# Channel norm of a convolution branch placed behind the fifth of eight attention half pairs of `w_out`, with the conv gates made ahead of it

## Chip, cores and metric

The kernel runs on one core of one Trainium2 chip. The metric is the device time of one execution in microseconds; 0.2% of it (4.4 us) is about what a measurement of this kernel can tell from no change. Engines are called PE (TensorE), DVE (VectorE), ACT (ScalarE), POOL (GpSimd) and SP (SyncE, which issues the weight loads). Every engine works through its own list of instructions in order.

## What is computed

The reference is two blocks on 256 tokens of width 2048, all in float32. The change lies in the first block, which has two layers. One layer, cut to what matters here:

```python
u = _rmsnorm(h, norm_g[i]) @ w_in[i]
a_val, a_glu, a_z, q, k, v, b_z = split(u)
y  = depthwise_conv31(a_val * sigmoid(a_glu)) + conv_b      # 1024 channels
ya = silu(layernorm_over_channels(y, cln_g, cln_b)) * silu(a_z)
yb = window_attention(q, k, v) * silu(b_z)                  # 1024 columns
h  = h + concat([ya, yb]) @ w_out[i]
e  = _rmsnorm(p[i] @ w_pe[i], pe_g[i])
h  = h + e * sigmoid(h @ w_pg[i])
```

The product with `w_out` has two halves of rows: the conv half needs `ya`, the attention half needs `yb` alone.

## The kernel before

Activations lie transposed, channels on partitions and 256 tokens along the free axis. Weights come from HBM in tiles of 4 x 128 rows by 256 columns (512 KB, SP). ACT rounds each to a high part (`whi`, L285), DVE forms the rest (`wlo`, L286), each from a pool of three buffers. Activations are kept as high and low parts as well (`Split`, `split_pair`, L271 and L272). `wide` makes one pair of output tiles: 16 k-tiles for `w_in`, 8 for one half of `w_out`. A half pair of `w_out` is thus two weight tiles: 16 matmuls of 512 columns (L353) and 16 of 256 (L355). `add_wide` (L368) adds the result to the residual `hT` in four DVE instructions.

A layer in program order: values and gates of the conv, keys, values, then four times queries, attention and two channel tiles of the convolution (30 DVE instructions each, L591, into `cy`); then the **channel norm**: `cs` sums the eight channel tiles over partitions on PE (L597), DVE subtracts the mean (L601), ACT squares (L603, L606), DVE adds (L607, L224), PE reduces to two columns (`pc`, L227), DVE makes the reciprocal root in thirteen small instructions (L207 to L214), copies it out (`rbx`, L246), PE transposes it (`rbp`, L249), ACT copies it to `rl` (L251). Then four z pairs of `w_in` with their `silu`, each followed by its two tiles of `cy` times `rl` (L616), `silu` (L619), times z (L621), split into `Y` (L271, L272). Then the eight attention half pairs of `w_out`, after every second of them one part of the embedding (`embed_part`: one weight tile of `w_pe`, 24 matmuls of 256 columns, L1231 to L1233, a square on ACT (L404), `ev` (L749) and a write of `ev` to the DRAM table `etab` by POOL, L750). Then `embed_scale` (`pc`, root and `rbp` of the embedding's own norm, into `re`), and the eight conv half pairs, which read `Y`.

The work isn't run in that order: the framework's scheduler places each instruction on its engine at build, by priorities that fall along the program's text (weight loads and splits are raised by `HP`). In the order before, the z pairs and the first four and a half attention half pairs stand ahead of the end of the convolution on PE. Below, "half pair a0 to a7" is an attention half pair, "b0" the first conv half pair, "e1 to e4" the four parts of the embedding.

Of the kernel before, what the change touches and what calls it, by code (L numbers as in the profile page):

```python
# [8 lines left out]
F32 = mybir.dt.float32  # L9
F32R = mybir.dt.float32r  # L10
I32 = mybir.dt.int32
AF = mybir.ActivationFunctionType
ALU = mybir.AluOpType
# [5 lines left out]
SEQ = 256  # L19
EPS = 1e-6  # L20
# [71 lines left out]
def bc(ap, n):  # L92

    p, x = ap.shape
    return ap.unsqueeze(1).to_broadcast([p, n, x])
# [21 lines left out]
class Kern:  # L117
# [395 lines left out]
    def layer1(self, i, S, st):  # L513
        nc, A = self.nc, self.A
        w_in = A["w_in"][i]
        kall = list(range(KD))
        if i == 0:
            rc, r = st
        else:
            rc = self.rs_cols(st["acc"], 1.0 / D, EPS, "rcl")  # L520
            r = self.bcast(rc[:], "r")
        r2 = bc(r[:], 2)
        cy = self.w1.tile([128, 8, SEQ], F32, tag="cy", name=self.nm("cy"))
# [13 lines left out]
        V = self.v1[i]  # L537
# [22 lines left out]
        Y = self.new_split()  # L560
        tail = None

        for j in range(4):
# [20 lines left out]
            for t in range(2):  # L584
                c = 2 * j + t
                cw = V["conv_w"][c]
                y = cy[:, c, :]
                ap = apads[j]
                nc.scalar.activation(y, ap[:, t, 0:SEQ], AF.Identity, scale=cw[:, 0:1], bias=V["conv_b"][:, c : c + 1])
                for k in range(1, 31):  # L590
                    prev, tail = tail, nc.vector.scalar_tensor_tensor(y, ap[:, t, k : k + SEQ], cw[:, k : k + 1], y, ALU.mult, ALU.add)  # L591
                    if k == 1 and prev is not None:
                        self.behind(tail, prev)

        ss = self.psum("o", [128, SEQ], "cs")
        for c in range(8):
            nc.tensor.matmul(ss[:], lhsT=self.ones, rhs=cy[:, c, :], start=(c == 0), stop=(c == 7))  # L597
        acc = self.wk.tile([128, 2, SEQ], F32, tag="acc", bufs=self.accb, name=self.nm("lnacc"))
        for c in range(0, 8, 2):
            y = cy[:, c : c + 2, :]  # L600
            nc.vector.scalar_tensor_tensor(y, bc(ss[:], 2), -1.0 / 1024, y, ALU.mult, ALU.add)  # L601
            if c == 0:
                nc.scalar.activation(acc[:], y, AF.Square)  # L603
            else:
                sq = self.w1.tile([128, 2, SEQ], F32, tag="sq", name=self.nm("sq"))
                nc.scalar.activation(sq[:], y, AF.Square)  # L606
                nc.vector.tensor_tensor(acc[:], acc[:], sq[:], ALU.add)  # L607
        rl = self.bcast(self.rs_cols(acc, 1.0 / 1024, EPS, "rc")[:], "rl", pool=self.w1)
        for j in range(4):
            pz = self.wide(w_in, 0, kall, 2048 + j * 256, S)  # L610
            zz = self.wk.tile([128, 2, SEQ], F32, tag="s", bufs=4, name=self.nm("z"))
            self.fold(zz, pz)
            nc.vector.tensor_tensor(zz[:], zz[:], r2, ALU.mult)
            nc.scalar.activation(zz[:], zz[:], AF.Silu)
            y = cy[:, 2 * j : 2 * j + 2, :]
            nc.vector.tensor_tensor(y, y, bc(rl[:], 2), ALU.mult)  # L616
            for t in range(2):
                c = 2 * j + t
                nc.scalar.activation(cy[:, c, :], cy[:, c, :], AF.Silu, scale=V["cln_g"][:, c : c + 1],  # L619
                                     bias=V["cln_b"][:, c : c + 1])  # L620
            nc.vector.tensor_tensor(y, y, zz[:], ALU.mult)  # L621
            self.split_pair(Y, 2 * j, y)

        for j in range(8):
            ps = self.wide(A["w_out"][i], 0, list(range(8, 16)), j * 256, Y)
            hh = self.at(self.hT, 2 * j, 2)
            self.add_wide(hh, ps)
            if j % 2:
                self.embed_part(i, j // 2, E)
        if self.dbg and f"yT{i}" in self.dbg:  # L630
            pass
        etab, re = E["tab"], self.embed_scale(E)
# [30 lines left out]
                self.stat_add(self.stf, hh, [self.fg[:, 2 * j + t : 2 * j + t + 1] for t in range(2)])  # L663
        self.dump_h(f"hT{i}")
        return N, st2

    def attend1(self, i, j, q, vd, gz, Y):
        nc = self.nc
# [917 lines left out]
```

## Time and profile before

| | us |
|---|---|
| median of 3 runs (2212.31 to 2216.68) | 2216.26 |
| the profiled execution, its own time | 2216.77 |
| its span | 2213.8 |
| PE busy in the span | 2168.2 (98%) |
| DVE busy | 1711.1 (77%) |
| ACT busy | 1207.7 (55%) |

The span starts at 0 with the first instruction; times of the trace are us from there, and some 3 us of the execution lie outside. The timeline merges neighbouring instructions of one line and gives in brackets how long the engine stood idle ahead of a row and what ended that. The windows give each engine's busy time in a stretch and the clock that TensorE was granted there, as a share of full speed.

### The profile page before, as it was taken

Reading aid. Unit: us, or ns where it says so; the run is one execution under the profiler, and the core shown is the slowest. Engines: PE = TensorE matmul, PEld = TensorE weight load, DVE = VectorE, ACT = ScalarE, POOL = GpSimd, SP = SyncE. Lnnn points to the kernel's source line nnn. Section 1 sums busy time; section 2 is a strip of 40 time slices with the busy share of each in tenths; the row PEclk is TensorE's granted clock in tenths of the full one; section 3 lists DMA queues with packets and bytes.
Section 4 is the critical chain, followed back from the end, with each engine's and each line's share of the span. In section 5 each row is a group of like instructions: output and inputs, shape, how many; then the busy total and the mean of one; then the engine's idle time right before and its main releaser. Section 6 shows DMA issues by size and latency. Waiting matters only on the chain.

```text
span 2213.8 us, 36348 instructions
## 1 busy us (share of the span) xinstructions
PE 2168.2 (98%) x13687; PEld 1935.8 (87%) x13687; DVE 1711.1 (77%) x3176; ACT 1207.7 (55%) x1861; POOL 106.4 (5%) x253
## 2 busy tenths in 40 slices
PE   8999999999999999999999999999999999999997
PEld 7899988888899878899999888888888888888887
DVE  6999999778989889787787877776765576556765
ACT  6456636565566546665666556455443444444443
POOL 3100000000000000001100000020000000000000
PEclk9999999999999999999999999999999999999999
DMA  8875556666665457677774435476666666566654
GB/s 238 240 211 164 173 162 209 194 207 189 188 183 170 149 166 219 212 214 216 221 183 123 129 88 158 157 255 203 191 189 192 194 189 190 190 196 188 189 190 140
DMA packets 374511, 412.76 MB, mean 186 GB/s; under 512 B 40456, under 2 KB 327429, under 8 KB 373952
## 3 DMA queue, kind: packets, MB, share of 16 engines
q1 hardware_dynamic: 336464, 366.06, 54.4%
q0 software_dynamic: 10960, 31.79, 4.6%
q10 hardware_dynamic: 26912, 12.60, 2.4%
q8 instruction: 107, 1.75, 0.3%
q14 instruction: 68, 0.56, 0.1%
HBM read 390.47 MB, written 19.92 MB: 185 GB/s over the span
## 4 chain that ended last, share of the span: by engine, by line
PE 91%; DVE 3%; DMA 2%; ACT 2%; issue 1%; ACTq 1%; SPq 0%; DVEq 0%
PE wide L353 35%; PE wide L355 18%; PE lin L328 4%; PE lin L327 4%; PE lin L329 4%; PE lin L1401 3%; PE lin L1402 3%; PE lin L1400 3%; PE dn L1402 2%; PE dn L1401 2%; PE dn L1400 2%; PE po L709 1%; DVE wlo L286 1%; PE lin L1231 1%; PE lin L1232 1%; PE lin L1233 1%
## 5 line engine op out<-in xcount | busy, mean ns | idle before, releaser
L285 ACT CAST whi<-wraw 128x1024 fp32r<-128x1024 f32 (+1 forms) x708 | 725.2, 1027 | 670.6 <-PE wide L353 290.8
L286 DVE TENSOR_TENSOR wlo<-wraw,whi 128x1024 fp32r<-128x1024 f32 (+1 forms) x708 | 843.4, 1192 | 313.6 <-ACT whi L285 307.0
L353 PE MATMUL wide<-xs,whi 128*128 128x512 f32 x3492 | 853.0, 393 | 6.0 <-ACT whi L285 3.7
L353 PEld LDWEIGHTS wide<-xs,whi 128*128 128x128 f32 x3492 | 638.0, 189 | 129.8 <-ACT whi L285 5.3
L355 PEld LDWEIGHTS wide<-xs,wlo 128*128 128x128 f32 x3492 | 454.2, 191 | 25.8 <-DVE wlo L286 5.5
L355 PE MATMUL wide<-xs,wlo 128*128 128x256 f32 x3492 | 466.3, 284 | 3.6 <-DVE wlo L286 3.6
L327 PE MATMUL lin<-xs,whi 128*128 128x256 f32 x844 | 241.1, 286 | 1.2 <-ACT whi L285 0.6
L329 PE MATMUL lin<-xs,wlo 128*128 128x256 f32 x844 | 240.2, 285 | 1.6 <-DVE wlo L286 1.6
L328 PE MATMUL lin<-xs,whi 128*128 128x256 f32 x844 | 240.2, 285 | 0.0
L591 DVE SCALAR_TENSOR_TENSOR cy<-apad,vc_cw,cy 128x256 f32<-128x256 f32 x480 | 229.6, 480 | 6.7
L327 PEld LDWEIGHTS lin<-xs,whi 128*128 128x128 f32 x844 | 161.5, 191 | 2.7 <-ACT whi L285 0.8
L329 PEld LDWEIGHTS lin<-xs,wlo 128*128 128x128 f32 x844 | 161.5, 191 | 2.4 <-DVE wlo L286 1.8
L328 PEld LDWEIGHTS lin<-xs,whi 128*128 128x128 f32 x844 | 161.6, 191 | 1.1 <-issue 0.7
L1401 PE MATMUL lin<-wlo,xs 128*128 128x512 f32 (+1 forms) x304 | 117.4, 386 | 0.5 <-DVE wlo L286 0.5
L1402 PE MATMUL lin<-whi,xs 128*128 128x512 f32 (+1 forms) x304 | 117.0, 385 | 0.0
L1400 PE MATMUL lin<-whi,xs 128*128 128x512 f32 (+1 forms) x304 | 113.7, 386 | 1.2 <-ACT whi L285 1.2
L1400 PEld LDWEIGHTS lin<-whi,xs 128*128 128x128 f32 x304 | 57.1, 188 | 12.8 <-ACT whi L285 1.6
L1401 PEld LDWEIGHTS lin<-wlo,xs 128*128 128x128 f32 x304 | 57.2, 188 | 11.9 <-DVE wlo L286 1.0
L1400 PE MATMUL dn<-whi,xs 128*128 128x512 f32 (+1 forms) x176 | 67.0, 381 | 0.0
L1401 PE MATMUL dn<-wlo,xs 128*128 128x512 f32 (+1 forms) x176 | 67.0, 381 | 0.0
L1402 PE MATMUL dn<-whi,xs 128*128 128x512 f32 (+1 forms) x176 | 67.0, 381 | 0.0
L1402 PEld LDWEIGHTS lin<-whi,xs 128*128 128x128 f32 x304 | 57.1, 188 | 11.1
(544 smaller groups left out, 2401.1 us busy)
## 6 DMA issues: line engine op xcount, KB each, us to landing
wraw<-in_w_in_dram SPq DMA_DIRECT2D x244, 512.0 KB, 4.1
wraw<-in_w_out_dram SPq DMA_DIRECT2D x89, 512.0 KB, 4.0
wraw<-in_ffn_w_gate_dram SPq DMA_DIRECT2D x88, 512.0 KB, 4.1
wraw<-in_ffn_w_up_dram SPq DMA_DIRECT2D x88, 512.0 KB, 3.9
wraw<-in_ffn_w_down_dram SPq DMA_DIRECT2D x87, 512.0 KB, 4.3
wraw<-in_w_pg_dram SPq DMA_DIRECT2D x64, 512.0 KB, 4.5
bt<-btab POOLq DMA_DIRECT2D x32, 192.0 KB, 3.1
btab<-bF ACTq DMA_DIRECT2D x4, 1024.0 KB, 8.1
```

Of the source, the lines that this page charges most:

```text
L285: nc.scalar.copy(hi[:], src)
L286: self.lo = nc.vector.tensor_tensor(lo[:], src, hi[:].bitcast(F32), ALU.subtract)
L327: nc.tensor.matmul(ps[:, t, :], lhsT=h, rhs=xh_, start=((t, k) == first), stop=False)
L328: nc.tensor.matmul(ps[:, t, :], lhsT=h, rhs=xl_, start=False, stop=False)
L329: nc.tensor.matmul(ps[:, t, :], lhsT=l, rhs=xh_, start=False, stop=((t, k) == last))
L353: nc.tensor.matmul(ps[t][:], lhsT=hi[:, i, ts], rhs=S.both(k).rearrange("p u c -> p (u c)"), **flags)
L355: nc.tensor.matmul(ps[t][:, :SEQ], lhsT=lo[:, i, ts], rhs=S.hi(k), **flags)
L591: prev, tail = tail, nc.vector.scalar_tensor_tensor(y, ap[:, t, k : k + SEQ], cw[:, k : k + 1], y, ALU.mult, ALU.add)
L709: nc.tensor.matmul(po[:, qb, g, :], lhsT=pT[:, kb, qb * 128 : qb * 128 + 128], rhs=vd[:, kb, j, :], start=(kb == 0), stop=(kb == 1))
L1400: nc.tensor.matmul(ps, lhsT=zh, rhs=hi, start=(k == 0), stop=False)
L1401: nc.tensor.matmul(ps, lhsT=zh, rhs=lo, start=False, stop=False)
L1402: nc.tensor.matmul(ps, lhsT=zl, rhs=hi, start=False, stop=(k == nt - 1))
```

## The change

The four z pairs move ahead of the norm, and their four gates stay in the four buffers of the tag `s`. The norm moves into a function, `channel_norm`, which the text calls behind attention half pair a4 (`j == 4`); applying it to `cy` (times `rl`, `silu`, times z, split) moves behind the last attention half pair and the last embedding part. No instruction of the arithmetic is added or dropped.

```diff
-        ss = self.psum("o", [128, SEQ], "cs")
...
-        rl = self.bcast(self.rs_cols(acc, 1.0 / 1024, EPS, "rc")[:], "rl", pool=self.w1)
+        zs = []
         for j in range(4):
             pz = self.wide(w_in, 0, kall, 2048 + j * 256, S)
...
             nc.scalar.activation(zz[:], zz[:], AF.Silu)
+            zs.append(zz)
+
+        for j in range(8):
+            ps = self.wide(A["w_out"][i], 0, list(range(8, 16)), j * 256, Y)
+            hh = self.at(self.hT, 2 * j, 2)
+            self.add_wide(hh, ps)
+            if j % 2:
+                self.embed_part(i, j // 2, E)
+            if j == 4:
+                rl = self.channel_norm(cy)
+        for j in range(4):
             y = cy[:, 2 * j : 2 * j + 2, :]
             nc.vector.tensor_tensor(y, y, bc(rl[:], 2), ALU.mult)
...
-            nc.vector.tensor_tensor(y, y, zz[:], ALU.mult)
+            nc.vector.tensor_tensor(y, y, zs[j][:], ALU.mult)
             self.split_pair(Y, 2 * j, y)
-
-        for j in range(8):
...
+    def channel_norm(self, cy):
+
+        nc = self.nc
+        ss = self.psum("o", [128, SEQ], "cs")
+        for c in range(8):
+            nc.tensor.matmul(ss[:], lhsT=self.ones, rhs=cy[:, c, :], start=(c == 0), stop=(c == 7))
...
+        return self.bcast(self.rs_cols(acc, 1.0 / 1024, EPS, "rc")[:], "rl", pool=self.w1)
```

In the changed program lines behind the edit have other numbers: the mean is L666, the squares L668 and L671, `cy` times `rl` L613, its `silu` L616, times z L618, the embedding matmuls L1239 to L1241, `ev` L757.

On PE in layer 0 the last channel sum `cs` (the one that needs the convolution's last instruction) stands, before, between the two halves of embedding part e2 (`lin_3547` and `lin_3567`):

```order
L1231 MATMUL lin_3547<-pp_2340,whi_3543 128x256
L1232 MATMUL lin_3547<-pp_2340,whi_3543 128x256
L1233 MATMUL lin_3547<-pp_2340,wlo_3544 128x256
L597 MATMUL cs_2834<-cy_261,cblk 128x256
L1231 MATMUL lin_3567<-pp_2340,whi_3543 128x256
L1232 MATMUL lin_3567<-pp_2340,whi_3543 128x256
```

and now inside embedding part e3 (`lin_3669`, `lin_3689`), behind half pairs a4 and a5:

```order
L1241 MATMUL lin_3669<-pp_2340,wlo_3666 128x256
L1240 MATMUL lin_3689<-pp_2340,whi_3665 128x256
L1241 MATMUL lin_3689<-pp_2340,wlo_3666 128x256
L1239 MATMUL lin_3689<-pp_2340,whi_3665 128x256
L662 MATMUL cs_3562<-cy_261,cblk 128x256
L1240 MATMUL lin_3689<-pp_2340,whi_3665 128x256
```

The same sum has moved behind half of e2, half of a4, all of a5 and 14 matmuls of e3. On PE in layer 0, at the end of the stretch, the last part of the embedding (`lin_3859`) is followed directly by the first conv half pair (`wide_3935`, `wide_3936`, which read `Y` as `xs_1330`) before:

```order
L1231 MATMUL lin_3859<-pp_2340,whi_3835 128x256
L1232 MATMUL lin_3859<-pp_2340,whi_3835 128x256
L1233 MATMUL lin_3859<-pp_2340,wlo_3836 128x256
L353 MATMUL wide_3936<-xs_1330,whi_3941 128x512 x2
L353 MATMUL wide_3935<-xs_1330,whi_3941 128x512 x4
```

and now there stand between them the embedding's `pc_3879` and two transposes, `rbp_3608` of the channel norm and `rbp_3901` of the embedding:

```order
L1240 MATMUL lin_3835<-pp_2340,whi_3811 128x256
L1241 MATMUL lin_3835<-pp_2340,wlo_3812 128x256
L227 MATMUL pc_3879<-cblk,acc_2343 128x1 x2
L249 MATMUL rbp_3608<-cblk,rbx_3606 128x128 x2
L249 MATMUL rbp_3901<-cblk,rbx_3899 128x128 x2
L189 MATMUL vps_4351<-cblk,vst_3906 128x124
L353 MATMUL wide_3935<-xs_1330,whi_3941 128x512 x2
```

Before, `rbp` of the channel norm stood ahead of a6 and the embedding's `pc` and `rbp` among the conv half pairs; the norm's own `pc` now stands right behind a7 in layer 0 and inside a7 in layer 1. On ACT in layer 0 the square of the norm's first pair (`lnacc`) stood before ahead of the square and the `ev` that read the embedding's `lin_3403` and `lin_3421`:

```order
L285 CAST whi_3613<-wraw_3591 128x1024
L603 ACTIVATE lnacc_2843<-cy_261 128x512
L404 ACTIVATE acc_2343<-lin_3403 128x512
L749 ACTIVATE ev_3416<-lin_3403,vc_a 128x256 x2
L606 ACTIVATE sq_2847<-cy_261 128x512
L606 ACTIVATE sq_2851<-cy_261 128x512
L285 CAST whi_3643<-wraw_3639 128x1024
```

and now the embedding's are ahead of it, and at the end of the stretch ACT has the norm's work in this order:

```order
L404 ACTIVATE sq_3849<-lin_3835 128x512
L757 ACTIVATE ev_3848<-lin_3835,vc_a 128x256 x2
L643 DMA e_4468<-etab_2344 128x512
L251 COPY rl_3611<-rbp_3608 128x256
L643 DMA e_4574<-etab_2344 128x512
L616 ACTIVATE cy_261<-cy_261,vc_b,vc_a 128x256 x8
L271 CAST xs_1330<-cy_261 128x2x256 x2
```

Two reads of `etab` into the buffers of `ev` now stand ahead of the eight `silu`, and the eight ahead of the first cast into `Y`. The order of SP's weight loads is as before; on POOL four writes of `etab` stand ahead of two small memsets that they stood behind.

## Rows read from the trace of the kernel before

**Rows 1.** The page: span; busy time, share and instructions by engine.
```profile
span 2213.8 us, 36348 instructions
PE 2168.2 (98%) x13687; PEld 1935.8 (87%) x13687; DVE 1711.1 (77%) x3176; ACT 1207.7 (55%) x1861; POOL 106.4 (5%) x253
```

**Rows 2.** Timeline, PE, layer 0: start, duration, line, operation, count [idle ahead, releaser].
```profile
325.61 0.74 PE L355 MATMUL wide<-xs,wlo 128*128 128x256 f32 x4 [1.02 <-DVE wlo L286]
...
327.10 0.28 PE L1231 MATMUL lin<-pp,whi 128*128 128x256 f32 x1
...
329.42 0.70 PE L597 MATMUL cs<-cy,cblk 128*128 128x256 f32 x2 [0.72 <-DVE cy L591]
332.78 0.39 PE L1231 MATMUL lin<-pp,whi 128*128 128x256 f32 x1 [2.66 <-ACT ev L749]
...
336.24 2.07 PE L353 MATMUL wide<-xs,whi 128*128 128x512 f32 x4 [0.92 <-ACT whi L285]
...
338.96 0.85 PE L227 MATMUL pc<-cblk,lnacc 128*128 128x1 f32 x4
...
350.18 0.38 PE L249 MATMUL rbp<-cblk,rbx 128*128 128x128 f32 x2
...
364.30 2.10 PE L353 MATMUL wide<-xs,whi 128*128 128x512 f32 x8
```

**Rows 3.** Timeline, ACT, layer 0.
```profile
330.88 0.63 ACT L603 ACTIVATE lnacc<-cy 128x512 f32<-128x512 f32 x1 [6.58 <-DVE cy L601]
```

**Rows 4.** Timeline, PE, layer 1.
```profile
808.50 0.74 PE L355 MATMUL wide<-xs,wlo 128*128 128x256 f32 x4 [1.02 <-DVE wlo L286]
809.07 1.08 PE L353 MATMUL wide<-xs,whi 128*128 128x512 f32 x4
...
814.68 0.58 PE L1231 MATMUL lin<-pp,whi 128*128 128x256 f32 x1 [2.66 <-ACT ev L749]
818.53 1.19 PE L353 MATMUL wide<-xs,whi 128*128 128x512 f32 x4 [0.92 <-ACT whi L285]
820.94 0.58 PE L227 MATMUL pc<-cblk,lnacc 128*128 128x1 f32 x4 [0.41 <-DVE lnacc L224]
...
846.64 1.63 PE L353 MATMUL wide<-xs,whi 128*128 128x512 f32 x6 [0.44 <-DVE xs L272]
```

**Rows 5.** Windows: stretch, length; busy of PE, PEld, DVE, ACT, POOL; PEclk, DMA share, GB/s.
```profile
333.00:341.00 8.00, 7.08 (x30) 6.23 (x30) 5.45 (x12) 5.10 (x10) 1.11 (x2) 0.57 0.32 110
814.00:818.00 4.00, 2.93 (x12) 2.63 (x12) 1.93 (x3) 2.35 (x5) 0.55 (x1) 0.57 0.17 66
1275.00:1285.00 10.00, 9.93 (x103) 9.51 (x104) 6.56 (x21) 6.29 (x16) 0.00 (x0) 0.66 0.33 105
0.00:4.00 4.00, 0.26 (x1) 0.18 (x1) 0.25 (x2) 0.55 (x1) 3.10 (x10) 1.00 0.41 96
```

**Rows 6.** Timeline, layer 0: durations of PE work and of DVE steps.
```profile
289.97 3.82 PE L353 MATMUL wide<-xs,whi 128*128 128x512 f32 x16
293.62 2.08 PE L355 MATMUL wide<-xs,wlo 128*128 128x256 f32 x16
...
341.11 0.16 DVE L213 TENSOR_TENSOR rs<-rs,rs 128x2 f32<-128x2 f32 x1
...
368.29 2.35 DVE L286 TENSOR_TENSOR wlo<-wraw,whi 128x1024 fp32r<-128x1024 f32 x2
```

**Rows 7.** Timeline, DVE and ACT, layer 0: the norm applied to `cy`.
```profile
351.52 2.50 DVE L616 TENSOR_TENSOR cy<-cy,rl 128x512 f32<-128x512 f32 x4 [0.29 <-ACT rl L251]
...
354.45 4.07 ACT L619 ACTIVATE cy<-cy,vc_b,vc_a 128x256 f32<-128x256 f32 x8
...
360.29 2.19 ACT L271 CAST xs<-cy 128x512 fp32r<-128x512 f32 x4
...
363.48 1.89 DVE L272 TENSOR_TENSOR xs<-cy,xs 128x512 fp32r<-128x512 f32 x3
```

**Rows 8.** The tile `etab`: its DMAs, issue to landing.
```profile
DMA to landing us min/median/max: 2.3/4.4/6.1
```

More of the change, by code (lines that the diff above doesn't have):

```diff
@@ L593, in layer1 @@
                         self.behind(tail, prev)
-        ss = self.psum("o", [128, SEQ], "cs")
[L596 to L607, printed above, removed]
-        rl = self.bcast(self.rs_cols(acc, 1.0 / 1024, EPS, "rc")[:], "rl", pool=self.w1)
+        zs = []
         for j in range(4):
@@ L620, in layer1 @@
                                      bias=V["cln_b"][:, c : c + 1])
-            nc.vector.tensor_tensor(y, y, zz[:], ALU.mult)
+            nc.vector.tensor_tensor(y, y, zs[j][:], ALU.mult)
             self.split_pair(Y, 2 * j, y)
-        for j in range(8):
[L625 to L629, printed above, removed]
         if self.dbg and f"yT{i}" in self.dbg:
@@ L665, in layer1 @@
         return N, st2
+    def channel_norm(self, cy):
[3 more added lines that the diff above has]
+            nc.tensor.matmul(ss[:], lhsT=self.ones, rhs=cy[:, c, :], start=(c == 0), stop=(c == 7))
+        acc = self.wk.tile([128, 2, SEQ], F32, tag="acc", bufs=self.accb, name=self.nm("lnacc"))
+        for c in range(0, 8, 2):
+            y = cy[:, c : c + 2, :]
+            nc.vector.scalar_tensor_tensor(y, bc(ss[:], 2), -1.0 / 1024, y, ALU.mult, ALU.add)
+            if c == 0:
+                nc.scalar.activation(acc[:], y, AF.Square)
+            else:
+                sq = self.w1.tile([128, 2, SEQ], F32, tag="sq", name=self.nm("sq"))
+                nc.scalar.activation(sq[:], y, AF.Square)
+                nc.vector.tensor_tensor(acc[:], acc[:], sq[:], ALU.add)
+        return self.bcast(self.rs_cols(acc, 1.0 / 1024, EPS, "rc")[:], "rl", pool=self.w1)
     def attend1(self, i, j, q, vd, gz, Y):
```

## The prediction

> **What bounds the kernel now.** I began with the page: PE is busy for 2168.2 of 2213.8 us [rows 1], so only PE's idle time and stretches at a lower clock can move the end, and any new wait of PE counts in full. Next I read PE's timeline around the channel norm, and the windows for its clock.
>
> In layer 0 PE waits four times within 12 us: 1.02, 0.72, 2.66 and 0.92 us, 5.3 in all [rows 2]. The 2.66 is the telling one. PE wants an accumulator for the second half of e2, and all three are held; the one that it gets is released by an `ev` on ACT, and ACT's list has the norm's first square ahead of that `ev`. ACT had been idle for 6.58 us until the mean was subtracted [rows 3]. So the wait is the convolution's end, handed on through ACT's order. Behind them the granted clock is 0.57 on the mean of 333 to 341 [rows 5] (first row). [...]
>
> **The change, part by part.**
>
> *The old waits.* Now the embedding's squares and `ev` stand ahead of the norm's square on ACT, so the 2.66 goes. The last channel sum stands behind 11.8 us more of PE work. Is the convolution done by then? DVE's list has 7.0 us of other work placed ahead of its end in layer 0: four `wlo` at 1.14 (the two of the last row take 2.35 [rows 6]), three adds of the embedding's squares at 0.6 (as the products of the same size in the first row of [rows 7]), two residual adds of half that size at 0.33. That moves its end from 329.4 to about 336.4, and PE arrives at 339.4 (by the steps below), 3 us later. In layer 1 it is 4.1 us of added work against 8 of PE's. I cost the old waits at nothing from here on. If this cover failed, each us beyond the 3 would go on PE one to one.
>
> *What is late next.* PE now has one place without cover: between e4 and b0. b0 reads `Y`, which needs the whole chain from the norm's `pc`: root, `rbx`, `rbp`, `rl`, products, `silu`, split. Before, that chain took from 338.96 to 364.30, 25.3 us in layer 0, and from 820.94 to 846.64, 25.7 in layer 1 [rows 2, 4], and a6, a7, e3, e4 and part of a5 lay under it. Now `pc` stands behind a7, or in its middle, and what is left to lie under the chain is e4 (and half of a7 in layer 1).
>
> *When `pc` runs.* A half pair is 16 matmuls of either kind, 5.7 us (289.97 to 295.70 [rows 6]); half an embedding part is 12 matmuls from 327.10 to 328.70, where the 0.72 begins [rows 2], so a whole one is about 3.0. In layer 0 e2 began at 327.10, or 326.1 without the 1.02 ahead of it. From there: e2 3.0, half of a4 2.85, a5 5.7, e3 3.0, the last sum 0.4, a6 5.7, a7 5.7, together 26.35. So `pc` is at about 352.4. (Six channel sums that stood earlier are now in the same stretch; PE comes to it earlier by as much.) In layer 1 e2 began at 809.98, 0.91 behind the row at 809.07 as in layer 0, or 808.96 without the wait; the same sum with a7 only to its middle (3.6) gives 833.2.
>
> *From `pc` to `rbx`.* The new order lists for DVE in layer 0, ahead of the root, a residual add and a `wlo` (1.5, from a7's end at 352.3, so 353.8) and then, to `rbx`: thirteen small ones at 0.2 (2.6; 0.16 in the third row of [rows 6], and a hand-over), two `wlo` (2.3), three adds of squares (1.8), a residual add and a fold (0.7), the embedding's first small one and `rbx` (0.5): 7.9, and `rbx` ends at 361.7. Two of the adds need e4's squares, which share one buffer; by ACT's list they are in time. In layer 1 the root begins at once, at 833.6; three `wlo`, two adds of squares, three residual adds and a fold make 8.8; e4 ends at 838.7, and its squares hold DVE for about 0.4: `rbx` at 842.8.
>
> *From `rbx` to b0.* `rbp` and `rl` take 0.4 each with a hand-over of 0.1. The products take 2.50 for four, the eight `silu` 4.07, the casts 2.19 for four, the low parts 1.89 for three [rows 7]. All eight `silu` stand ahead of the first cast, and b0 needs the first pair's two parts. In layer 0: `rl` at 362.8; seven small ones on DVE to 363.1; first product 363.7; eight `silu` to 367.8; the last product with z 368.4, some small ones with the embedding's `rbx` 0.5, first low part 0.6: b0 at 369.5. ACT also holds two reads of `etab` here, which wait for writes to land, 4.4 us at the median [rows 8]: the second is free at about 363.9, nearly hidden. In layer 1 `rl` is at 843.8, two `silu` end at 845.5, the second read holds ACT to 846.0, six `silu` to 849.1, then 0.6 for z, 0.2, 0.6: b0 at 850.5.
>
> b0 comes at 369.5 instead of 364.30 (+5.2) and at 850.5 instead of 846.64 (+3.9): **+9.1 us**. These differences already contain what the old waits gave back.
>
> *The clock.* Behind the new waits, some 11 to 13 us with almost no matmuls, PE may start at the lower level. [...] Against it stands the start of the span, where PE is busy for 0.26 of 4 us and the clock is 1.00 [rows 5] (fourth row). Bounds 0 and 3.4 a layer; I take 2.5, the mean of the three, since they lie inside the running program as these waits will: **+5.0**. [...]
>
> *The rest.* SP's loads keep their order. POOL's moved writes free `ev` buffers earlier and nobody waits for the two memsets behind them. The embedding's root, now ahead of b0 and not among the conv half pairs, gives DVE room in a stretch where PE has no wait to lose. Weights of b0 and half of b1 are split before b0 begins, and b1's other half has 8 us. All nothing.
>
> Sum: 9.1 + 5.0 = 14.1 on the profiled 2216.77, which is 0.5 over the median: 2216.3 + 14.1 = **2230.4, say 2230**.
>
> **Rivals.**
>
> *The new wait only equals the old ones.* The shortest chain that the order allows: PE's `rbp` stands behind the embedding's `pc`, which needs e4's squares. e4 ends at 355.8; square 0.6, add 0.7, fold 0.4, `pc` 0.5, `rbp` and `rl` 0.8, product 0.6, eight `silu` 4.1, cast and low part 1.1: 364.6, +0.3; layer 1 838.7 + 8.8 = 847.5, +0.9. Without a clock penalty 2217. It needs DVE to reach each step without queueing, and its list has `wlo` between them.
>
> *Faster.* If the chain were fully covered, b0 would follow e4 and its `pc` at once: 356.4 and 839.3, which is -7.9 and -7.3: 2201. For it speaks that the old waits do go; against it that nothing stands on PE between e4 and b0. It decides from the point where `rbp` is free before e4 ends, and the order forbids that.
>
> *The chain takes as long as before*, 25.3 and 25.7, because the `wlo` and the writes hold it up as they did: b0 at 377.7 and 858.9, +13.4 and +12.3, 2242 without the clock and up to 2249 with it. Against it: the old chain had four half pairs' `wlo` and adds among its steps, the new has two to four `wlo`.
>
> *The change doesn't do what it says.* The order shows the moves, so this needs no case of its own; it would end at 2216, with the first rival.
>
> **How the numbers follow.** Forecast 0.63 (its own range 2223 to 2238), equal 0.15, covered 0.05, as long as before 0.17. Slower by over 0.2%, that is above 2220.7, holds the forecast but for a little, all of the last case and a little of the equal one: 0.80. Within 0.2% 0.14, faster 0.06. The range runs from 2216, which leaves out the covered case and a third of the equal one, to 2241, which leaves out half of the last: 0.18 outside.
>
> **What would show it.** Right: no wait above 1 us at `cs` or for an `ev`; `pc` near 352 and 833; one PE wait of 9 to 14 us, in pieces around `pc` and `rbp`, ahead of b0 in each layer, released by DVE's low part of `Y`; clock 0.50 behind it. Wrong: b0 before 364 or 846 (the sum's root and `silu` steps too long), a PE wait at the last `cs` (the convolution late), or the clock at 1.00 behind the wait.

## The result, and the profile after

The changed kernel takes 2233.11 us at the median of four runs (2228.62 to 2236.43), the kernel before beside it 2215.79. The ratio is 1.0080 with a 95% interval of 1.0058 to 1.0101: slower by 0.8%, or 17 us. A second measurement on another chip, among the experiments below, gives 2228.70 and 1.0062 (1.0046 to 1.0079). The prediction was 2230, with 2216 to 2241 as its range.

The profiled execution of the changed kernel has a span of 2232.3 us. The page's first part, after:

```profile
span 2232.3 us, 36342 instructions
PE 2173.8 (97%) x13687; PEld 1941.5 (87%) x13687; DVE 1715.5 (77%) x3176; ACT 1208.3 (54%) x1861; POOL 106.5 (5%) x253
```

The span grew by 18.5 us against [rows 1] and PE's busy time by 5.6: some 13 us are new waits, less the old ones that went, and the rest is the same work at a lower clock.

The timeline of PE in layer 0, after (start, duration, line, operation, count, idle ahead and its releaser; a row without brackets had no idle time ahead), answers to [rows 2]:

```profile
340.11 0.60 PE L662 MATMUL cs<-cy,cblk 128*128 128x256 f32 x2
...
352.69 0.50 PE L227 MATMUL pc<-cblk,lnacc 128*128 128x1 f32 x4
...
360.33 0.98 PE L227 MATMUL pc<-cblk,acc 128*128 128x1 f32 x4 [4.15 <-DVE rc L214]
361.76 0.69 PE L249 MATMUL rbp<-cblk,rbx 128*128 128x128 f32 x2 [0.45 <-DVE rbx L246]
370.39 0.69 PE L249 MATMUL rbp<-cblk,rbx 128*128 128x128 f32 x2 [7.94 <-DVE rbx L246]
...
370.99 5.30 PE L353 MATMUL wide<-xs,whi 128*128 128x512 f32 x12
```

The same in layer 1, beside [rows 4]:

```profile
840.37 0.50 PE L227 MATMUL pc<-cblk,lnacc 128*128 128x1 f32 x4
...
849.46 0.58 PE L227 MATMUL pc<-cblk,acc 128*128 128x1 f32 x4 [3.50 <-DVE rc L214]
849.90 0.41 PE L249 MATMUL rbp<-cblk,rbx 128*128 128x128 f32 x2
858.54 5.46 PE L353 MATMUL wide<-xs,whi 128*128 128x512 f32 x12 [8.23 <-DVE rs L213]
```

The waits of [rows 2] and [rows 4] are gone. In their place PE stands idle for 12.5 us in layer 0 and 11.7 in layer 1 between e4 and b0, in the pieces that the prediction named: ahead of the embedding's `pc`, of `rbp`, and of b0. (In layer 0 the last piece is booked on the embedding's `rbp`, which stands ahead of b0 on PE; b0 itself could start 0.6 us later.) The windows (length; busy of PE, PEld, DVE, ACT, POOL; granted clock, DMA share, GB/s) show what the waits leave behind, beside [rows 5]:

```profile
333.00:341.00 8.00, 8.00 (x53) 7.30 (x53) 7.04 (x13) 2.51 (x3) 0.18 (x2) 1.00 0.61 190
365.00:370.00 5.00, 0.00 (x0) 0.00 (x0) 3.47 (x10) 4.63 (x10) 0.00 (x0) 0.50 0.18 53
370.00:375.00 5.00, 4.61 (x13) 3.68 (x14) 4.14 (x9) 1.74 (x4) 0.00 (x0) 0.50 0.00 0
375.00:380.00 5.00, 5.00 (x29) 4.43 (x28) 2.03 (x3) 1.05 (x1) 0.00 (x0) 0.91 0.05 9
855.00:860.00 5.00, 1.46 (x4) 1.20 (x5) 4.94 (x15) 4.06 (x9) 0.00 (x0) 0.50 0.09 31
860.00:865.00 5.00, 5.00 (x20) 4.13 (x19) 0.54 (x2) 0.96 (x1) 0.00 (x0) 0.60 0.00 0
```

The stretch that had 0.57 before is at 1.00 with PE busy throughout. Behind the new waits b0 begins at 0.50, the lowest clock of these windows; its twelve wide matmuls take 5.30 us there in layer 0, where sixteen take 3.82 in [rows 6]. What that costs is an estimate from the windows, PE's busy time by what the clock lacked of 1.00: in layer 0 0.50 of 4.61 us and 0.09 of 5.00, in layer 1 0.50 of 1.46 and 0.40 of 5.00, or 2.8 and 2.7 us.

Where the 18.5 us went is best read from the start of the same instructions in both traces. The tile views of three groups in the changed kernel (duration in ns min/median/max, first and last start in us):

```profile
L738 PE MATMUL ppt<-cblk,pr x8: 272/272/273, 253.5 to 738.8; 128*128 128x128 f32 x8
L227 PE MATMUL pc<-cblk,acc x20: 167/250/352, 360.3 to 1011.2; 128*128 128x1 f32 x20
L1370 PE MATMUL htr<-cblk,xt x32: 270/272/299, 1510.0 to 1531.6; 128*128 128x128 f32 x32
```

and in the kernel before:

```profile
L730 PE MATMUL ppt<-cblk,pr x8: 272/272/273, 252.4 to 730.6; 128*128 128x128 f32 x8
L227 PE MATMUL pc<-cblk,acc x20: 164/250/250, 376.5 to 997.2; 128*128 128x1 f32 x20
L1362 PE MATMUL htr<-cblk,xt x32: 270/272/273, 1492.1 to 1513.5; 128*128 128x128 f32 x32
```

`ppt` starts ahead of the changed stretch of layer 0 (first) and ahead of that of layer 1 (last), the last `pc` of an `acc` and `htr` enclose the second block's mixer, which the edit doesn't touch. Differences of such starts, kernel less kernel before, give this table; all rows below come from the same three views of each kernel and its span. Each row is a single profiled execution, and some of these lie well below their kernel's median: gates alone by 5.6 us, by pairs by 3.3, adds on POOL by 2.7, the last row by 8.3. "To 252" is the shift with which a trace comes to layer 0; the shift at layer 1 is that and the column of layer 0.

| kernel | to 252 | layer 0 | layer 1 | mixer, 997 to 1492 | rest | span |
|---|---|---|---|---|---|---|
| the change | +1.1 | +7.1 | +5.8 | +3.9 | +0.6 | +18.5 |
| the change, second trace | -0.8 | +5.0 | +5.9 | +2.3 | +0.7 | +13.1 |
| gates alone | -0.6 | -0.1 | +0.7 | -0.3 | -0.3 | -0.6 |
| no root | +1.4 | -5.1 | -7.1 | +14.7 | +1.2 | +5.1 |
| late root | -0.5 | +4.9 | +4.7 | -0.9 | +1.4 | +9.6 |
| by pairs | +1.2 | +4.5 | +4.6 | -1.5 | -0.9 | +7.9 |
| late and by pairs | +1.8 | +4.1 | +2.9 | +0.7 | 0.0 | +9.5 |
| norm behind a2 | 0.0 | +4.1 | +3.4 | +11.2 | +1.4 | +20.1 |
| behind a2, late, by pairs | +1.1 | +3.4 | +2.8 | 0.0 | -0.1 | +7.2 |
| adds on POOL | -0.8 | +4.3 | +5.1 | -1.6 | -0.9 | +6.1 |
| short chain, behind a4 | +1.4 | +2.3 | -4.3 | -0.9 | +3.2 | +1.7 |
| short chain, old place | +0.6 | -4.6 | -5.2 | +2.7 | -1.2 | -7.7 |
| the same, 128 columns | -0.4 | +0.1 | -5.2 | -1.5 | -1.0 | -8.0 |

The two layers cost 12.9 us in this trace and 10.9 in the second one. The mixer adds 3.9 that the prediction hadn't.

### The profile page after: what moved, and what is told of

The parts are those of the page before. It is cut to its first block, busy times and chain, and to the rows that moved or that the text cites. A ratio compares the mean times of both kernels' runs of the same rounds, so it can differ in the third digit from the quotient of the medians.

```text
span 2232.3 us, 36342 instructions
## 1 busy us (share of the span) xinstructions
PE 2173.8 (97%) x13687; PEld 1941.5 (87%) x13687; DVE 1715.5 (77%) x3176; ACT 1208.3 (54%) x1861; POOL 106.5 (5%) x253
## 3 DMA queue, kind: packets, MB, share of 16 engines
q8 instruction: 107, 1.75, 0.3%
## 4 chain that ended last, share of the span: by engine, by line
PE 91%; DMA 3%; DVE 2%; issue 2%; ACT 2%; ACTq 1%; POOL 0%; SPq 0%; POOLq 0%; DVEq 0%
PE wide L353 35%; PE wide L355 18%; PE lin L328 4%; PE lin L327 4%; PE lin L329 4%; PE lin L1409 3%; PE lin L1410 3%; PE lin L1408 3%; PE dn L1409 2%; PE dn L1410 2%; PE dn L1408 2%; PE po L717 1%; PE lin L1241 1%; PE lin L1239 1%; PE lin L1240 1%
## 5 line engine op out<-in xcount | busy, mean ns | idle before, releaser
L286 DVE TENSOR_TENSOR wlo<-wraw,whi 128x1024 fp32r<-128x1024 f32 (+1 forms) x708 | 844.0, 1193 | 327.6 <-ACT whi L285 318.9
L353 PEld LDWEIGHTS wide<-xs,whi 128*128 128x128 f32 x3492 | 643.0, 190 | 138.1 <-issue 10.8
L1408 PEld LDWEIGHTS lin<-whi,xs 128*128 128x128 f32 x304 | 57.1, 188 | 13.1 <-ACT whi L285 2.0
```

Of the source, the lines that this page charges most:

```text
L286: self.lo = nc.vector.tensor_tensor(lo[:], src, hi[:].bitcast(F32), ALU.subtract)
L353: nc.tensor.matmul(ps[t][:], lhsT=hi[:, i, ts], rhs=S.both(k).rearrange("p u c -> p (u c)"), **flags)
L1408: nc.tensor.matmul(ps, lhsT=zh, rhs=hi, start=(k == 0), stop=False)
```

## The experiments

Theory: the loss is the chain from the norm's `pc` to b0, which now has only e4 under it, and the lower clock behind the wait. Rivals: it is the gates' move, the convolution's end, DVE's load, or a stage further on. Times are medians, with the ratio to the kernel before on the same chip and its 95% interval; 0.2% is about the least that can be told.

| kernel | us | ratio |
|---|---|---|
| the change, second time | 2228.70 | 1.0062 (1.0046 to 1.0079) |
| gates alone | 2220.93 | 1.0015 (1.0003 to 1.0027) |
| no root | 2219.77 | 1.0012 (1.0000 to 1.0024) |
| late root | 2226.68 | 1.0058 (1.0039 to 1.0078) |
| norm behind a2 | 2233.29 | 1.0075 (1.0058 to 1.0093) |
| by pairs | 2226.78 | 1.0049 (1.0033 to 1.0066) |
| late and by pairs | 2225.66 | 1.0041 (1.0025 to 1.0056) |
| behind a2, late, by pairs | 2222.25 | 1.0027 (1.0015 to 1.0040) |
| adds on POOL | 2224.65 | 1.0030 (1.0018 to 1.0042) |
| short chain, behind a4 | 2216.39 | 1.0000 (0.9984 to 1.0015) |
| short chain, old place | 2206.97 | 0.9966 (0.9952 to 0.9981) |
| the same, 128 columns | 2215.89 | 0.9995 (0.9983 to 1.0006) |

### Gates alone

```diff
+            zs.append(zz)
+        rl = self.channel_norm(cy)
+        for j in range(4):
+            y = cy[:, 2 * j : 2 * j + 2, :]
...
         for j in range(8):
             ps = self.wide(A["w_out"][i], 0, list(range(8, 16)), j * 256, Y)
```

> One half of the change alone: the four conv gates are made ahead and kept in their tiles, but the norm and the products behind it stand ahead of the attention rows of w_out, as in the kernel before. Theory (the norm's place costs it all): 2211 to 2220, the time of the kernel before; the wait of 2 to 3 us for an accumulator of e2 is there again, b0 comes at 364 to 366 and 846 to 848, and no wait of more than 2 us stands ahead of b0. Its order in the mixer of the third layer is that of the kernel before, so by order as by chance the clock may be 1.00 from 1350 to 1390. Rival (the gates cost it): gates that are made early put 5 us or more of PE and DVE work ahead of the convolution's end or hold the four buffers that they share with the attention's scores, and the time is 2226 to 2236.

Layer by layer it is the kernel before (-0.1 and +0.7 us), and its PE timeline has the old wait again, on the same releaser as [rows 2]:

```profile
331.54 0.39 PE L1238 MATMUL lin<-pp,whi 128*128 128x256 f32 x1 [2.66 <-ACT ev L756]
```

The median is 3.5 us above the kernel before (1.0015), less than the 0.2% that can be told. The profiled execution is the fastest of the ten (2215.30), so its trace can't say where those 3.5 us are. The gates' move costs at most that; the rest of the 0.6 to 0.8% comes with the norm's place.

### No root

```diff
-            nc.vector.tensor_tensor(y, y, bc(rl[:], 2), ALU.mult)
+            nc.vector.tensor_tensor(y, y, r2, ALU.mult)
```

> The changed kernel, but the products behind the norm use a scale that is there already (that of the layer's input) in place of the norm's root, so that nothing on the way to b0 waits for the channel sum's column, the root or their broadcast; mean, products, silu, gates and split stay. Left out is the norm's root in the result. Theory (the uncovered chain is the loss): PE's waits ahead of b0, 12.5 us in layer 0 and 11.7 in layer 1, go but for 0 to 2 us each, and with them the clock's fall behind them, worth 2 to 3 us each: 2233 - 24 - 5 = 2204, between 2199 and 2209. Rival (most of the loss lies elsewhere, in DVE's load or the clock): over 2215, with b0 at 364 or later in layer 0.

By the time the theory missed by 16 us. By the layers it held: without the chain they are 5.1 and 7.1 us faster than before and 12 to 13 us each faster than the change, and the trace is 10.8 us ahead of the kernel before at the start of the mixer. There 14.7 us are lost, in a stage whose arithmetic is the same. The windows from the last `pc` of an `acc` to the first `htr`, over the same 3798 matmuls, in the kernel before:

```profile
997.20:1492.10 494.90, 480.32 (x3798) 441.17 (x3798) 387.97 (x987) 288.42 (x518) 45.79 (x104) 0.99 0.58 170
```

and without the root:

```profile
986.40:1496.00 509.60, 489.77 (x3798) 448.39 (x3798) 388.61 (x987) 288.89 (x518) 45.78 (x104) 0.97 0.56 164
```

PE is idle for 5.3 us more and takes 9.4 more for its work, at 0.97 instead of 0.99. The scheduler orders the whole program at once: from the middle of PE's list on this kernel differs from the one before in 37 places, the change in 10, the gates alone in 2. The same thing strikes the norm behind a2 (38 places, 11.2 us).

### The change again, and the mixer's 4 us

> The changed kernel itself, once more, for its trace. What I want from it is the third loss: in the first trace of the changed kernel the stretch from 1364 to 1384 us, in the mixer of the third layer, had a granted clock of 0.80 and from 1384 to 1404 of 0.94, where the kernel before has 1.00 in the same stretch, and some 4 us went there. Theory A (order): the new program's order in that stretch, which differs from before in a few instructions, brings the clock down each time; then the second trace has it again at the same place, and the time is 2233 +-4. Theory B (chance): where the clock falls in that stretch differs from run to run; then the second trace has 1.00 there or a fall elsewhere, and the times spread from 2226 to 2237. The waits of 12.5 and 11.7 us ahead of b0, and a clock of 0.50 to 0.6 for some 5 us behind them, come again by both.

The loss came again, so the count of two traces spoke for the order. Other kernels speak against it: the late root, the one by pairs and the one with adds on POOL have the order of the change through this stretch but for two small matmuls, which they place as the kernel before does, and lose nothing. The same work in windows of 4 us, change:

```profile
1372.00:1376.00 4.00, 3.29 (x31) 2.53 (x29) 3.72 (x12) 3.50 (x13) 0.00 (x0) 1.00 0.20 73
1376.00:1380.00 4.00, 4.00 (x25) 3.43 (x25) 4.00 (x12) 1.90 (x5) 0.00 (x0) 0.50 0.00 0
1380.00:1384.00 4.00, 3.48 (x13) 2.81 (x12) 2.21 (x5) 1.53 (x4) 0.00 (x0) 0.50 0.01 4
```

and by pairs:

```profile
1367.00:1371.00 4.00, 3.29 (x34) 2.59 (x32) 3.71 (x13) 3.70 (x14) 0.00 (x0) 1.00 0.21 66
1371.00:1375.00 4.00, 3.48 (x36) 2.92 (x33) 4.00 (x12) 2.51 (x8) 0.00 (x0) 1.00 0.00 0
1375.00:1379.00 4.00, 4.00 (x26) 3.57 (x26) 3.94 (x8) 3.00 (x4) 0.00 (x0) 1.00 0.02 4
```

PE has such gaps in both (3.29 busy of the first 4 us in each), and behind them the clock falls in one trace and not in the other. The version with the short chain in the old place has the fall too (0.56 from 1350 to 1360), and its sister with 128 columns not. So in this stage the clock falls in some traces and holds in others with almost the same work; what decides it is open. It is worth 2 to 4 us in the two traces of the change, and the three other kernels with the norm behind a4 and this order do without it.

### Late root

The embedding's root is held behind the last low part of the conv rows, and the first two reads of `etab` behind the last cast.

```diff
+        ycast, ylow = self.cast, self.low
         etab, re = E["tab"], self.embed_scale(E)
+        self.behind(self.half, ylow)
...
-            nc.scalar.dma_start(e[:], etab[:, 2 * j : 2 * j + 2, :])
+            read = nc.scalar.dma_start(e[:], etab[:, 2 * j : 2 * j + 2, :])
+            if j < 2:
+                self.behind(read, ycast)
```

> The changed kernel, but the embedding's root begins behind the last low part of the conv rows, and ACT's first two reads of the embedding table stand behind their last cast. It takes away what stands beside the chain to b0: the embedding's column sum and broadcast on PE ahead of b0, its root on DVE, the two reads ahead of silu on ACT. Theory (these stand in the chain's way): in layer 0 the first silu begins within 1.0 us of the first product and not 2.5 us later, and b0 1.5 to 5 us earlier than 370.99 (365.9 to 369.5); in layer 1 rl is copied within 0.6 us of rbp and not 2 us later, and b0 1 to 3 us earlier; together 2225 to 2231. Rival (the root, its low parts and the silu are the chain, the rest rides beside it): b0 within 0.7 us of where it was, 2233 +-3.

ACT in layer 0, in the change:

```profile
362.49 0.37 ACT L251 COPY rl<-rbp 128x256 f32<-128x256 f32 x1 [3.46 <-PE rbp L249]
364.99 0.33 ACTq L643 DMA_DIRECT2D e<-etab  x1
365.37 4.04 ACT L616 ACTIVATE cy<-cy,vc_b,vc_a 128x256 f32<-128x256 f32 x8 [2.51 <-DMA etab<-ev]
```

and with the late root:

```profile
360.06 0.37 ACT L251 COPY rl<-rbp 128x256 f32<-128x256 f32 x1 [2.67 <-PE rbp L249]
361.19 4.04 ACT L616 ACTIVATE cy<-cy,vc_b,vc_a 128x256 f32<-128x256 f32 x8 [0.76 <-DVE cy L613]
```

The second table read held the `silu` by 1.75 us (2.51 less 0.76). PE at b0 in layer 0, in the second trace of the change and with the late root:

```profile
368.21 4.11 PE L353 MATMUL wide<-xs,whi 128*128 128x512 f32 x12
```

```profile
366.70 5.02 PE L353 MATMUL wide<-xs,whi 128*128 128x512 f32 x12 [6.68 <-DVE xs L272]
```

In layer 1 b0 is at 854.89 and 853.05. Less the shift that each trace brings with it, it comes 1.8 and 2.0 us earlier with the late root, as the theory said. Yet layer 0 is only 0.1 us shorter and layer 1 1.2: the clock behind the wait stayed low for longer (from 370 to 371 us it was 0.50 with the late root and 0.72 in the second trace; b0's first twelve wide matmuls took 5.02 us and not 4.11 in layer 0, 5.46 and not 4.74 in layer 1).

### By pairs, and both together

```diff
+            if j > 1:
+                self.behind(pr, gated[j - 2])
...
+                if j > 1:
+                    self.behind(si, casts[j - 2])
```

> The changed kernel, but the tail of the norm is ordered by pairs: the silu of pair 2 stands behind the cast of pair 0 on ACT, that of pair 3 behind the cast of pair 1, and DVE's products by rl likewise behind the products by z. Theory (all eight silu ahead of the first cast are a term of the chain): b0's first matmul 1.5 to 2.5 us earlier than 368.2 to 371.0 in layer 0 and than 854.9 to 858.5 in layer 1; part of it is given back inside b0, which then waits for pairs 2 and 3; 2225 to 2231. Rival (b0 is held by the embedding's broadcast and table reads, and not by silu): b0 within 0.7 us of where it was, 2229 to 2234. The third loss, at 1364 to 1404 us: the order there is that of the changed kernel; if that order brings the clock down, the granted clock is under 0.9 there again, as in two traces of the changed kernel; if it is chance, it may be 1.00, as in the run with the late root, which has the same order.

b0 is at 369.28 and 854.83: against the second trace (368.21 and 854.89) 0.9 us earlier in layer 0 and 1.6 in layer 1, each less the shift between the two traces, 2.0 and 1.5. That is at the lower edge of what the theory named or below it, and the time (2226.78) is within its range.

> Both together: the embedding's root and table reads behind the conv rows' tail, and the tail by pairs. Theory (the terms add): b0 at 364.5 to 366 in layer 0, 1 to 2 us ahead of the 366.70 with the late root alone, and at 851 to 852.5 in layer 1 instead of 853.05; 2222 to 2228. The waits ahead of b0 stay at 8 us or more a layer, since the root with three low parts among its steps stays. Rival (what b0 gains it loses to the lower clock behind the wait, since that comes back at a time of its own): b0 earlier as said, but the shift of everything behind b0 no smaller than with the late root alone, 4.8 and 5.1 us a layer; 2225 to 2230.

b0 comes at 367.80 and 853.15, which less the shifts is 1.2 and 1.4 us earlier than with the late root alone, and PE still waits for 10.3 and 9.1 us. The layers go from 4.9 and 4.7 to 4.1 and 2.9: the terms add, in part. The two orderings take 4 us from the change, and the root with the low parts among its steps stays.

### The norm behind a2

```diff
-            if j == 4:
+            if j == 2:
                 rl = self.channel_norm(cy)
```

> The changed kernel with one number changed: the norm is called behind the third of the eight half pairs (a2), not behind the fifth (a4). By the new order the last channel sum then stands near the end of a5, the norm's column sum pc in the middle of e3, and rbp near the end of a7, so that e3's second half, half of a6, a7 and e4, 13 us of PE work, lie under the chain from pc to b0, in place of e4's 3. Theory (the loss is the chain's missing cover): pc at 341 to 343 instead of 350.7 to 352.7, the chain takes 17 to 22 us since more low parts of weights stand among its steps, b0 at 359 to 365, PE's wait ahead of b0 3 to 8 us and not 12; layer 1 likewise; 2211 to 2221, near the time of the kernel before. Rival (the convolution isn't done so early, and waits at the last channel sum or for an accumulator held by an ev behind the norm's squares take the place): waits of 3 us or more around a5 in each layer, 2222 to 2232.

The time is 1.3 us above the rival's range, and for the most part not for its reason: the layers cost 7.5 us and not 11 to 13, and 11.2 are in the mixer with its other order, as above. In the layers the theory held in part. PE's wait ahead of b0 was 6.63 us in each, within the theory's 3 to 8. But `pc` came at 345.62 in layer 0 and not at 341 to 343, behind two new waits of PE, 2.56 us for a low part of weights and 0.95 for the norm's adds: waits where the rival had looked for them, by other releasers. With late root and pairs as well:

> All three: norm behind a2, late root and reads, tail by pairs. Theory (cover plus a shorter chain): b0 at 356 to 361 in layer 0, PE's wait ahead of it 0 to 4 us, 2203 to 2213, faster than the kernel before by 0.2 to 0.6%. Rival (the chain isn't shorter, or waits at the channel sum take the place): 2215 or more.

This missed as well. PE in layer 0 of the combined version:

```profile
342.71 0.74 PE L355 MATMUL wide<-xs,wlo 128*128 128x256 f32 x4 [2.56 <-DVE wlo L286]
...
346.76 0.61 PE L227 MATMUL pc<-cblk,lnacc 128*128 128x1 f32 x4 [0.95 <-DVE lnacc L224]
...
356.91 0.38 PE L249 MATMUL rbp<-cblk,rbx 128*128 128x128 f32 x2
...
366.05 5.46 PE L353 MATMUL wide<-xs,whi 128*128 128x512 f32 x12 [5.42 <-DVE xs L272]
```

`pc` comes 6 us earlier than in the change and has e3's second half, half of a6, a7 and e4 under it, but the chain from `pc` to b0 has grown from 18.3 (352.69 to 370.99) to 19.3 us, since six low parts of weights (1.22 us each, three of them ahead of `rbx`) and the embedding's adds stand among its steps on DVE, where the change had three low parts. More cover is partly eaten by what the cover itself puts on DVE.

### Adds on POOL

```diff
-            self.stat_add(E["st"], pe[:])
...
+                nc.scalar.activation(sq[:], pe[:], AF.Square)
+                nc.gpsimd.tensor_tensor(st["acc"][:], st["acc"][:], sq[:], ALU.add)
```

> The changed kernel with one thing moved: the seven adds of the embedding's squares (0.68 us each) run on POOL and not on DVE. Three of them stand among the root's steps in layer 0, two in layer 1. Theory (the chain from pc to b0 is as long as DVE's list makes it): the list is 2.0 us shorter there in layer 0 and 1.4 in layer 1, b0 comes 1.5 to 3.5 us earlier than 368.2 to 371.0 and 1 to 3 us earlier than 854.9 to 858.5, and the time is 2224 to 2230. Rival (POOL is slow at it, over 1.5 us an add, and the one buffer of squares then holds e4's accumulators and the embedding's column sum, which stands ahead of b0 on PE in layer 0): b0 no earlier, 2231 to 2238.

The layers cost 4.3 and 5.1 us. b0 is 1.9 us earlier than in the second trace in layer 0 and, less the shift, 1.0 in layer 1, and the time within the theory's range. The rival has a part: an add takes POOL 1.28 to 2.28 us, and the embedding's `pc` now waits for these adds, which is 4.6 us of PE's waits in each layer.

### The short chain

Late root, by pairs, adds on POOL, and the norm's squares in the convolution's input tiles with one column sum over all four, so that neither DVE's adds nor the one buffer of squares lies on the chain:

```diff
-                nc.vector.tensor_tensor(acc[:], acc[:], sq[:], ALU.add)
+            ap = apads[c // 2][:, :, 0:SEQ]
+            nc.scalar.activation(ap, y, AF.Square)
...
+        for b in range(2):
+            for c in range(8):
+                nc.tensor.matmul(pc[:, b : b + 1], lhsT=sqs[c // 2][:, c % 2, b * 128 : b * 128 + 128], rhs=self.ones[:, 0:1],
+                                 start=(c == 0), stop=(c == 7))
```

> The norm stays behind a4, and everything that I found in the chain's way is taken out: adds of the embedding's squares on POOL, the norm's squares written into the convolution's input tiles, which are free by then, with the column sum taken by PE from all four (no adds, no shared buffer), the embedding's root and table reads behind the tail, the tail by pairs. Theory (the loss is the chain's length against its cover, and the length is DVE's list): from the last channel sum to pc 6 to 9 us in place of 12.6, rbp within a7 in place of behind e4, PE's wait ahead of b0 0 to 3 us in layer 0 and 0 to 2 in layer 1, b0 at 356 to 360 and 840 to 845; 2201 to 2211, faster than both kernels. Rival (the place behind a4 can't be covered): a wait of 5 us or more stays in each layer, 2216 or more.

Layer 1 did what was expected: no wait of PE, 4.3 us less than before. Layer 0 has one wait of 3.61 us at b0 (366.53), because `rbp` stands late in PE's list (at 356.27, with its input ready at 352.3). And the time, 2216.39, is 5 us over the top of the range. PE and the windows there:

```profile
344.41 2.96 PE L683 MATMUL pc<-cblk,apad 128*128 128x1 f32 x20
347.23 1.63 PE L353 MATMUL wide<-xs,whi 128*128 128x512 f32 x3
```

```profile
346.00:348.00 2.00, 2.00 (x9) 1.90 (x10) 0.52 (x4) 0.00 (x0) 1.21 (x10) 0.50 0.89 198
350.00:352.00 2.00, 2.00 (x11) 2.00 (x11) 1.49 (x4) 0.00 (x0) 0.00 (x0) 0.50 0.00 0
```

PE isn't idle, and the clock is at 0.50 to 0.58 from 346 to 353, and again from 830.5 to 834 in layer 1. The first fall came while the 32 matmuls of one column were running (342.72 to 347.37, a few others among them), the second 1 us behind them (825.84 to 829.47).

> The same shorter chain, but the norm stands ahead of the attention rows, as in the kernel before. Theory (with a short chain the place matters little, since the convolution's end decides where the sum can stand): last channel sum in the middle of a5, pc in e3, rbp in a6, b0 without a wait over 1 us; no wait for an accumulator, since the embedding's squares don't share a buffer with the norm's any more; 2199 to 2209, within 4 us of the version behind a4. Rival (in this place the last channel sum meets an unfinished convolution, since PE no longer waits ahead of it): a wait of 2 us or more at the channel sum in each layer, 2210 to 2217.

With the same chain in the old place PE waits for nothing from 318 to 372 and from 800 to 870, and the kernel is faster than both: 2206.97, 0.9966 (0.9952 to 0.9981). The place does matter, against what I wrote: 9 us between the two, measured on the same chip. The last channel sum stands at 334.5 and `pc` at 340.25, `rbp` at 350.1 and b0 at 360.4, 3.9 us ahead of [rows 2].

### One column and 128 columns

```diff
-        pc = self.psum("o", [128, 2], "pc")
+        pc = self.psum("o", [128, 2, 128], "pc")
...
-                nc.tensor.matmul(pc[:, b : b + 1], lhsT=sqs[c // 2][:, c % 2, b * 128 : b * 128 + 128], rhs=self.ones[:, 0:1],
+                nc.tensor.matmul(pc[:, b, :], lhsT=sqs[c // 2][:, c % 2, b * 128 : b * 128 + 128], rhs=self.ones[:, 0:128],
...
-        rc = self.rsqrt(pc[:], 1.0 / 1024, EPS, "rc")
+        rc = self.rsqrt(pc[:, :, 0], 1.0 / 1024, EPS, "rc")
```

> The version before this with the norm ahead of the attention rows and the short chain, with one number changed: the 32 matmuls of the norm's column sum have 128 equal columns on their moving side in place of one (only the first column of the result is read). In the three traces with such sums, PE was busy without a gap and the granted clock still fell to 0.50 to 0.58 right behind the 32 one-column matmuls, at 344 to 348 us, at 346 to 353 and at 830 to 834, and once it didn't. Theory (one-column matmuls count as little work for the clock, so that a burst of them acts like a wait): with 128 columns the clock is 1.00 behind the sums in both layers; each matmul takes as long as before, 0.11 us, to within 0.03; the time is 0 to 4 us less than 2207, at 2203 to 2207. Rival (it is chance, or it goes with what else is done there): the clock falls to 0.6 or less behind the sum of one layer or both again, 2205 to 2211. rbp stands ten matmuls later in the order than before, so a wait of up to 2 us ahead of b0 would be no surprise.

PE and the granted clock with one column, the norm in the old place:

```profile
340.25 3.63 PE L682 MATMUL pc<-cblk,apad 128*128 128x1 f32 x32
344.76 3.34 PE L353 MATMUL wide<-xs,whi 128*128 128x512 f32 x8
```

```profile
342.00:344.00 2.00, 2.00 (x19) 2.00 (x20) 0.08 (x1) 0.00 (x0) 1.59 (x9) 1.00 0.77 229
344.00:346.00 2.00, 2.00 (x9) 1.76 (x9) 1.69 (x13) 1.17 (x2) 0.12 (x2) 0.56 0.57 205
346.00:348.00 2.00, 2.00 (x7) 1.56 (x6) 2.00 (x3) 1.11 (x3) 1.54 (x1) 0.58 0.06 24
```

and with 128:

```profile
339.25 3.73 PE L682 MATMUL pc<-cblk,apad 128*128 128x128 f32 x32
343.55 2.01 PE L353 MATMUL wide<-xs,whi 128*128 128x512 f32 x8
361.57 5.46 PE L353 MATMUL wide<-xs,whi 128*128 128x512 f32 x12 [3.61 <-DVE xs L272]
```

```profile
340.00:350.00 10.00, 10.00 (x69) 9.20 (x69) 7.15 (x21) 3.98 (x7) 5.07 (x12) 1.00 0.58 195
```

The sum takes as long (3.73 against 3.63 us) and the clock holds, here and in layer 1 (1.00 from 820 to 830). That is the theory's side; one trace with and one without can't exclude chance, and in layer 1 the clock had held with one column too. The time did not follow: the median, 2215.89, is above both ranges. In the trace `rbp` went ten matmuls further back and PE came to b0 sooner, so that a wait of 3.61 us stands there, and with it the lower clock, 0.66 from 360 to 370. But this execution took 2207.55, as much as the profiled one with one column (2207.86), and the median is 8 us above it. What the other ten executions lost is in no trace. Their clock over the run is lower, 0.990 to 0.994 where the profiled one has 0.996.

## Why the prediction was right

*What bounds it, and the old waits at nothing.* Right: PE has no wait at the last channel sum, at 340.11 (339.4 predicted, and this trace is 1.1 us late from its start), and 1.00 is the clock where it was 0.57. The cover was counted closely too: the convolution's last instruction ends on DVE at 337.62, or 336.5 less the 1.1 (336.4 predicted), 2.5 us ahead of PE. One reading of the order was a little off, which changes nothing: 16 matmuls of e3, not 14, stand ahead of the moved sum.

*`pc`, root, `rbx`.* Less the 1.1 us by which this trace is late, `pc` is at 351.6 (352.4 predicted), the root starts at 353.3 (353.8), `rbx` is done at 360.6 (361.7) and `rl` at 361.8 (362.8). In layer 1 `pc`, less the 8.2 of this trace there, is at 832.2 (833.2). In layer 1 `rbx` is done at 849.71, or 841.5 (842.8). All came 0.5 to 1.3 us sooner than counted, and the steps between them are right to 0.6: the count of DVE's list carried the forecast.

*From `rl` to b0.* b0 is at 370.99, or 369.9 less the shift (369.5), and 858.54, or 850.3 less the 8.2 (850.5). The way there was not as priced. In layer 0 the second table read, called nearly hidden, set the start of the `silu`: it came free at 364.99, or 363.9 less the shift, just as predicted, but `rl` was 1.0 us sooner than counted and had to wait for it. The 1.75 us of hold is for the most part that lead, which bought nothing; the first `silu` began at 365.37, or 364.3 (363.7). In layer 1 the first read, not priced at all, held `rl` itself (`rbp` had ended at 850.31):

```profile
851.82 0.37 ACT L251 COPY rl<-rbp 128x256 f32<-128x256 f32 x1 [3.67 <-DMA etab<-ev]
```

So `rl` was done at 852.19, or 844.0 (843.8), in spite of the early `rbx`, and the second read, priced at 0.5, held nothing. That b0 came out to 0.4 us is thus in part luck: steps counted too long and holds counted too short met. What released b0 was the first low part of `Y`, as predicted: it ended at 370.94 and 858.40, and the rows name the embedding's instructions that stood beside it.

*The waits' sum.* Layer 0 costs 7.1 us with its clock, where 5.2 + 2.5 = 7.7 was predicted, layer 1 5.8 where it was 3.9 + 2.5 = 6.4. In the second trace it is 5.0 and 5.9; the 2.1 between the two in layer 0 are 0.8 of the silu's hold (2.51 and 1.71 us) and the rest clock (b0's twelve wide matmuls took 5.30 and 4.11 us).

*The clock.* 2.8 and 2.7 us by the estimate above, against 2.5 each. No run shows the 2.5 us a layer that the forecast adds; what the runs showed in its place is b0 beginning at 0.50, after 12.5 and 11.7 us of idle PE in pieces, at that estimated cost. (The same estimate makes 3.0, 1.3 and 3.4 us of the first three rows of [rows 5], 2.6 on the mean.) The row of the span's start, the other bound, was of no use for a wait inside the program.

*Not foreseen.* The mixer's 3.9 us. I had looked at the order behind the two layers and not at its timing, since the instructions are the same. The profiled run would have been 14 us over before by my terms and is 17.3 over by its time; the medians are 17.3 and, on the other chip, 11.2 us over. That the forecast lies as near as 3 us is partly luck: one loss was left out, the layers were counted 1.2 us too dear, and 1.7 of the trace's 18.5 us lie in stretches that the edit doesn't touch (ahead of 252 us and behind the mixer).

*Rivals.* "Only equals the old ones" and "covered" fell with the 12.5 and 11.7 us of wait; "as long as before" (25 us from `pc` to b0) with 18.3 and 18.2. That the chain was the loss is shown by taking it away: without the root the layers are 5.1 and 7.1 us faster than before, where the covered case had said 7.9 and 7.3.

## What to carry to other kernels

A step that is moved to sit under other work has to be priced by its whole chain against the work that is left under it: here 18 us of chain against 3 of cover. The place could be paid for by shortening the chain on the engine that it queues on (adds to an idle engine, no shared buffer, the foreign root and reads out of its way), and then the old place was the better one, 2206.97 against 2216.39 us on one chip. Its gain is not yet safe: with 128 columns, on another chip, the same version was no faster than the kernel before (0.9995). An edit near the top of a scheduled program can reorder a stage far behind it, at 11 to 15 us in two cases here, so the order of the whole program is to be compared and a mark set in the trace ahead of and behind each stage before a time is put down to the edit.

## What the runs showed of the hardware that I had not expected

- The granted clock fell to 0.50 to 0.58 for some 3.5 to 7 us with PE busy throughout, three times: twice about 1 us or less behind 32 matmuls of one column in 3.6 us, and once while such matmuls ran, spread over 4.7 us. A fourth time, with two other matmuls among them, it didn't fall. With 128 columns, at 3.73 us for the 32 against 3.63, it stayed at 1.00 in both layers. With one trace of each version, chance isn't excluded.
- The clock fell behind similar gaps of PE in some traces and not in others: 0.50 from 1376 to 1384 in the change, 1.00 over the same work by pairs. Within one kernel the time goes in part with the clock's mean over the run: the kernel before takes 2211.8 to 2218.7 us in executions at 0.994 and 2215.8 to 2222.2 at 0.990 to 0.992.
- When b0 came 1.8 us earlier behind a wait (late root), it began at 0.50 all the same, and the clock rose no earlier: it was at 1.00 from 372 us on, and from 371 on in the second trace of the change. Of the gain 0.1 us was left in layer 0.
- An add of 128 by 512 on POOL takes 1.56 us on the mean of 14 (1.28 to 2.81), where DVE takes 0.68. DVE was busy throughout beside an add of 1.28 us (326.32, adds on POOL) and one of 2.28 (355.99), so what stretches it is open.
